# Scan phase of a hybrid SSD and Conformer block: decay weights shared with ScalarE, weight rows loaded earlier, and the first modulation vector and five gate pairs moved between phases

## The chip, the cores and the metric

The kernel runs on one core of one Trainium2 chip. The metric is the time of one execution on the device in microseconds (us); the time of a kernel is the median of its runs. The profile comes from one profiled execution.

## The reference

One layer of a diffusion backbone: 256 latent tokens and 256 context tokens of width 2048, float32. The parts that matter here:

```python
proj = h @ w_in                     # split into z, xbc, dt_raw, glu, gates
xbc = jax.nn.silu(dwconv_seq(xbc, conv_w, conv_b))
dt = jax.nn.softplus(dt_raw + dt_bias)
...
    cs = jnp.cumsum(da_c, axis=1)                 # in a chunk of 128 tokens
    seg = cs[:, :, None] - cs[:, None, :]
    decay = jnp.exp(jnp.where(lower, seg, -jnp.inf))
    cb = jnp.einsum("blgn,bsgn->blsg", c_c, b_c)
    y_diag = jnp.einsum("blsgj,bsgjp->blgjp", cb[..., None] * decay, xdt_c)
    y_off = jnp.einsum("blgn,bgjpn->blgjp", c_c, h) * jnp.exp(cs)[..., None]
...
y_a = rmsnorm(y * jax.nn.silu(z), ssm_norm) @ w_proj_a
y_b = cf @ w_proj_b                               # cf: the Conformer branch
x = x + g1 * ((sigmoid(g_a) * y_a + sigmoid(g_b) * y_b) @ w_out)
x = x + g2 * swiglu(modulate(rmsnorm(x, norm_ffn), sh2, sc2))
```

The scan runs forward and backward over the tokens, for 8 groups of 8 heads (64 wide, state 128). The six modulation vectors (shift, scale and gate of each sub-layer) are `silu(c) @ w_mod + b_mod`; the two that the first input needs are made in phase 0, the other four (g1, sh2, sc2, g2; 2048 numbers each) are those called `modvec(0)` to `modvec(3)` below.

## The kernel before

**Weight stream.** Weights come in tiles of 512 KB (`w32`, L102), issued on SP's queue in program order into 6 buffers. `split` (L109) makes two tiles of each: `wh`, a rounded copy by ScalarE (ACT, L113), and `wl`, the rest, by VectorE (DVE, L114). A tile is a "unit": for a pair of column tiles TensorE (PE) runs 16 matmuls on it (L151 with 512 columns, L153 with 256), or 24 with 512 columns where context and latents are both needed (L143, L144, L146). `wh` and `wl` have 4 buffers each. The program is scheduled ahead of time; each engine then runs its instructions in a fixed order, in which the two halves of `split` have a raised priority.

**Phases.** Phase 0 (to about 250 us) norms, modulates and makes the first projections. Phase A (to about 932 us) is the scan. Phase B (to about 1295 us) makes 16 pairs of the Conformer input (`f`) and 16 gate pairs (8 for `ga`, 8 for `gb`); phase C multiplies by w_proj_b and w_proj_a; D by w_out (to about 1672 us), E and F are the feed-forward part.

**Phase A.** A loop over 8 stages; stage s scans group s-1 with `ssd` (L533) and meanwhile runs projections: `bcpair` and `xpair` of later groups, `zpair` (L689) of groups whose scan is finished. `ssd` is a generator of 15 steps; the loop takes a step each time that the projections' running time, by a table of estimates, has passed the next fifteenth. In the last stage the steps are spread over all units but the last 8. In `ssd`, `diag` (L607) makes the weights of half the heads of a chunk: `cs` (512 KB, the cumulative sums sent to all partitions by a DMA, 2 buffers) is shifted by ACT (L614) and by DVE (L617, which also takes the minimum of the two directions), ACT takes the exponential (L619), POOL and DVE make `w` from the products C·B of both directions (L621, L624), and L626 multiplies. PE then uses it (L633, `ydiag`), and L662 to L669 add the carried state, scaled by `ec` (another broadcast DMA), to `yfm`. `zpair` gates `yfm` with z, adds the squares to `yss` on POOL (L701), scales by `ssm_norm` on DVE (L703) and writes `yg` to DRAM.

**The modulation vectors.** `modvec` (L480) loads 32 tiles of w_mod (the "rows") through the same 6 buffers and adds each to `mac` on DVE (L489, L491), without PE. A hook after each unit takes its steps: `modvec(0)` 34 steps in 116 units of phase A, `modvec(1)` and `modvec(2)` 68 steps in 246 units of B, C and D, `modvec(3)` in phase E.

Of the kernel before, what the change touches and what calls it, by code (L numbers as in the profile page):

```python
# [62 lines left out]
def _block(top, tc, nc, x, c, ctx_in, c_ctx, w_mod, b_mod, norm_mix, w_in, conv_w, conv_b,  # L63
# [162 lines left out]
    def xct():  # L226
        return pa1.tile([P, 512], F32, tag="xc", name="xc", bufs=8)
# [24 lines left out]
    cst = pa1.tile([P, 2, P], F32, name="cst")  # L252
    ncs = pa1.tile([P, 2, 64], F32, name="ncs")
# [4 lines left out]
    def dt_chain(dt_raw, scr):  # L258
# [44 lines left out]
        V.tensor_copy(out=cst.rearrange("p a b -> p (a b)"), in_=b[:, 0:256])  # L303
        V.tensor_scalar(out=ncs, in0=cst[:, :, 0:64], scalar1=-1.0, scalar2=None, op0=ALU.mult)
# [175 lines left out]
    def modvec(slot, pl):  # L480
        """One of the other four modulation vectors, off the tensor engine; a step per unit."""
        o = slot + 2
        for h in range(D // UB):
            ac = pl.tile([P, UB], F32, tag="mac", name="mac", bufs=1)
            for k in range(KD):
                c0 = o * D + h * UB
                wt = w32([(lambda t: t, w_mod[k * P:(k + 1) * P, c0:c0 + UB])])
                if k == 0:
                    V.tensor_scalar(out=ac, in0=wt, scalar1=silc[:, k:k + 1], scalar2=None, op0=ALU.mult)  # L489
                else:  # L490
                    V.scalar_tensor_tensor(out=ac, in0=wt, scalar=silc[:, k:k + 1], in1=ac, op0=ALU.mult, op1=ALU.add)  # L491
                yield
            yield
# [26 lines left out]
    # ------------------------------------------------------------ phase A  # L520
    with pool("pa2", "right") as pa:
# [11 lines left out]
        def ssd(g, xts, Bt, Ct, res):  # L533
            """The two scans of group g, a step per yield; the output goes feature-major to res."""
            gs = slice(8 * g, 8 * g + 8)
            csb, ecb = {}, {}

            def cs_load(cc, half):
# [4 lines left out]
                csb[cc, half] = t  # L543
# [545 lines left out]
```

## Time and profile before

| | us |
|---|---|
| median of 3 runs | 2440.6 |
| lowest and highest run | 2436.62, 2441.51 |
| span of the profiled execution | 2437.1 |
| TensorE busy in it | 2355.9 |
| VectorE busy | 1672.2 |
| ScalarE busy | 1194.6 |
| GpSimd busy | 153.2 |

The span runs from the first to the last instruction of the profiled execution. Its own time is that span, as far as the profile shows it, and it lies 3.5 us under the median and inside the runs. The difference between the span and TensorE's busy time, 81.2 us, is all the time in which TensorE stands idle.

### The profile page before, as it was taken

The page shows a single profiled execution, that of the slowest core. Times are in us where ns is not written, and L with a number is a line of the kernel's source. Part 1 is how long each engine was busy: PE and PEld are TensorE (multiplying, and loading weights), DVE is VectorE, ACT ScalarE, POOL GpSimd, SP SyncE. Part 2 cuts the span into 40 slices and gives each one's busy share as a digit, 9 for nine tenths or more (in the row PEclk, how much of TensorE's full clock was granted, in tenths as well). Part 3 has the DMA queues.
Part 4 walks back from the last instruction along what each step waited for, and adds up shares of the span by engine and source line. Part 5 has one row for each costly group of instructions (what it writes and reads, how often), then busy time and mean ns, then how long its engine had stood idle before and what let it go on. Part 6 is the DMA issues. An engine that isn't in the chain of part 4 may idle for free.

```text
span 2437.1 us, 35157 instructions
## 1 busy us (share of the span) xinstructions
PE 2355.9 (97%) x13400; PEld 1981.7 (81%) x13400; DVE 1672.2 (69%) x2343; ACT 1194.6 (49%) x1700; POOL 153.2 (6%) x181
## 2 busy tenths in 40 slices
PE   6999899999999999999999999999999999999998
PEld 3668687878777778888888888887888888888888
DVE  4659887877777887878757666667666566655554
ACT  4335546546444565545755444445444444444443
POOL 1000010100100111013000000000000000000000
PEclk9999999999999999999999999999999999999999
DMA  9994556655655567776777777785777677766663
GB/s 274 292 298 116 133 170 182 180 156 166 182 155 159 178 195 238 237 238 208 234 249 250 241 252 237 242 264 182 232 221 226 214 226 229 219 197 193 194 192 113
DMA packets 468458, 509.41 MB, mean 209 GB/s; under 512 B 18148, under 2 KB 438195, under 8 KB 467777
## 3 DMA queue, kind: packets, MB, share of 16 engines
q1 hardware_dynamic: 461936, 488.74, 65.5%
q0 software_dynamic: 5792, 17.35, 2.2%
q8 instruction: 105, 1.72, 0.3%
q10 hardware_dynamic: 560, 1.08, 0.1%
q14 instruction: 65, 0.52, 0.1%
HBM read 496.35 MB, written 10.75 MB: 208 GB/s over the span
## 4 chain that ended last, share of the span: by engine, by line
PE 76%; DMA 4%; DVE 4%; issue 2%; ACT 1%; SPq 0%; POOL 0%; DVEq 0%; ACTq 0%; POOLq 0%
PE acc L151 38%; PE acc L153 21%; PE acc L143 4%; PE acc L146 4%; PE acc L144 3%; DMA w<-in_w_mod_dram 2%; PE acc L155 2%; DMA cs<-cs_d 2%; DVE wl L114 2%; PE ss L662 1%; PE ss L633 1%; DVE xc L245 0%; PE tp L556 0%; PE ss L641 0%; ACT wh L113 0%
## 5 line engine op out<-in xcount | busy, mean ns | idle before, releaser
L114 DVE TENSOR_TENSOR wl<-w,wh 128x1024 fp32r<-128x1024 f32 (+3 forms) x702 | 839.4, 1200 | 412.9 <-ACT wh L113 411.3
L113 ACT CAST wh<-w 128x1024 fp32r<-128x1024 f32 (+3 forms) x702 | 717.8, 1024 | 728.0 <-PE acc L151 450.1
L151 PE MATMUL acc<-hx,wh 128*128 128x512 f32 x1556 | 433.8, 397 | 0.0
L151 PE MATMUL acc<-h,wh 128*128 128x512 f32 x1320 | 366.7, 396 | 4.4 <-DVE h L973 2.4
L151 PEld LDWEIGHTS acc<-hx,wh 128*128 128x128 f32 x1556 | 272.4, 189 | 41.8 <-issue 3.4
L153 PEld LDWEIGHTS acc<-hx,wl 128*128 128x128 f32 x1664 | 255.0, 188 | 38.3 <-DVE wl L114 1.8
L143 PE MATMUL acc<-hx,wh 128*128 128x512 f32 x656 | 267.8, 409 | 3.0 <-ACT wh L113 2.4
L153 PE MATMUL acc<-hx,wl 128*128 128x256 f32 x1664 | 267.4, 282 | 1.4 <-DVE wl L114 1.4
L491 DVE SCALAR_TENSOR_TENSOR mac<-w,silc,mac 128x1024 f32<-128x1024 f32 x120 | 156.5, 1304 | 162.8 <-DMA w<-in_w_mod_dram 162.4
L151 PEld LDWEIGHTS acc<-h,wh 128*128 128x128 f32 x1320 | 231.5, 190 | 38.2 <-issue 5.3
L144 PE MATMUL acc<-hx,wh 128*128 128x512 f32 x656 | 259.9, 397 | 0.0
L153 PEld LDWEIGHTS acc<-h,wl 128*128 128x128 f32 x1408 | 216.1, 189 | 30.1
L153 PE MATMUL acc<-h,wl 128*128 128x256 f32 x1408 | 223.9, 281 | 0.0
L146 PE MATMUL acc<-hx,wl 128*128 128x512 f32 x656 | 185.2, 395 | 0.0
L151 PE MATMUL acc<-hid,wh 128*128 128x512 f32 x602 | 166.3, 396 | 0.0
L143 PEld LDWEIGHTS acc<-hx,wh 128*128 128x128 f32 x656 | 124.3, 190 | 39.9 <-issue 8.5
L146 PEld LDWEIGHTS acc<-hx,wl 128*128 128x128 f32 x656 | 124.5, 190 | 27.2 <-issue 0.4
L144 PEld LDWEIGHTS acc<-hx,wh 128*128 128x128 f32 x656 | 124.9, 190 | 25.9 <-issue 2.1
L151 PE MATMUL acc<-yg,wh 128*128 128x512 f32 x496 | 136.4, 395 | 0.4 <-ACT wh L113 0.4
L151 PEld LDWEIGHTS acc<-hid,wh 128*128 128x128 f32 x602 | 103.6, 189 | 13.8
L153 PEld LDWEIGHTS acc<-hid,wl 128*128 128x128 f32 x616 | 94.3, 189 | 13.1
L153 PE MATMUL acc<-hid,wl 128*128 128x256 f32 x616 | 98.0, 281 | 0.0
(346 smaller groups left out, 2722.7 us busy)
## 6 DMA issues: line engine op xcount, KB each, us to landing
w<-in_w_in_dram SPq DMA_DIRECT2D x248, 512.0 KB, 4.5
w<-in_w_mod_dram SPq DMA_DIRECT2D x192, 512.0 KB, 4.8
w<-in_w_ffn_gate_dram SPq DMA_DIRECT2D x88, 512.0 KB, 4.6
w<-in_w_ffn_up_dram SPq DMA_DIRECT2D x88, 512.0 KB, 4.6
w<-in_w_ffn_down_dram SPq DMA_DIRECT2D x88, 512.0 KB, 3.5
w<-in_w_proj_a_dram SPq DMA_DIRECT2D x64, 512.0 KB, 4.7
w<-in_w_in_dram SPq DMA_DIRECT2D x74, 256.0 KB, 3.8
cs<-cs_d SPq DMA_DIRECT2D x32, 512.0 KB, 6.0
```

Source lines behind the costliest of these rows:

```text
L113: A.copy(out=hi[:, :n], in_=t[:, :n])
L114: V.tensor_tensor(out=lo[:, :n], in0=t[:, :n], in1=hi[:, :n].bitcast(F32), op=ALU.subtract)
L143: E.matmul(o, wj(hi, k), act(kofs + k)[:, 0, :ncol], start=kofs + k == kbeg, stop=False)
L144: E.matmul(o, wj(hi, k), act(kofs + k)[:, 1, :ncol], start=False, stop=False)
L146: E.matmul(o, wj(lo, k), act(kofs + k)[:, 0, :ncol], start=False, stop=last and k == nk - 1)
L151: E.matmul(o2, wj(hi, k), act(kofs + k)[:, :, :T], start=kofs + k == kbeg, stop=False)
L153: E.matmul(o[:, :T], wj(lo, k), act(kofs + k)[:, 0, :T], start=False, stop=last and not hold)
L155: E.matmul(o2, wj(hi, nk - 1), act(kofs + nk - 1)[:, :, :T], start=False, stop=True)
L491: V.scalar_tensor_tensor(out=ac, in0=wt, scalar=silc[:, k:k + 1], in1=ac, op0=ALU.mult, op1=ALU.add)
L633: E.matmul(ydp[r:r + 64, (hd // 2) * P:(hd // 2 + 1) * P], xs[:, cc, hd * 64:(hd + 1) * 64], e[:, j * P:(j + 1) * P], start=True, stop=True)
L662: E.matmul(yo[:, i * P:(i + 1) * P], hs_[r][:, i * P:(i + 1) * P], Ct[:, cc * P:(cc + 1) * P], start=True, stop=True)
```

## The change

- `diag`: ACT shifts both directions (8 instructions of 128x128 in place of 4), DVE takes the minimum in one instruction of 128x512 in place of four (was L617). The products of the backward direction go to a tile `w2` by four ACT instructions, and DVE adds `w` and `w2` in one 128x512 instruction in place of four (was L624).
- `zpair`: the sum `yss` moves from POOL to DVE (16 instructions), the scaling by `ssm_norm` from DVE to ACT (32).
- `cs` of the next group is loaded as soon as the second chunk of a group frees its buffer, not at the group's start; `ec_load(0)` is issued at the start of `ssd`; `diag(1, 0)` is written two steps later.
- `modvec` loads a row one step ahead of the one that it adds. `modvec(0)` leaves phase A; B, C and D now take 102 steps in 226 units.
- z of group 4, 5 and 6 is made a stage sooner (stages 6, 7, 8), and five of the `ga` pairs (20 units) are made in stages 7 and 8 instead of in phase B; `xc` gets a ninth buffer, since their results lie there until phase B's tiles exist.

```diff
 def modvec(slot, pl):
...
-            for k in range(KD):
-                c0 = o * D + h * UB
-                wt = w32([(lambda t: t, w_mod[k * P:(k + 1) * P, c0:c0 + UB])])
-                if k == 0:
-                    V.tensor_scalar(out=ac, in0=wt, scalar1=silc[:, k:k + 1], scalar2=None, op0=ALU.mult)
-                else:
-                    V.scalar_tensor_tensor(out=ac, in0=wt, scalar=silc[:, k:k + 1], in1=ac, op0=ALU.mult, op1=ALU.add)
+            c0 = o * D + h * UB
+            wn = None
+            for k in range(KD + 1):
+                wt = wn
+                if k < KD:
+                    wn = w32([(lambda t: t, w_mod[k * P:(k + 1) * P, c0:c0 + UB])])
+                if k == 1:
+                    V.tensor_scalar(out=ac, in0=wt, scalar1=silc[:, 0:1], scalar2=None, op0=ALU.mult)
+                elif k > 1:
+                    V.scalar_tensor_tensor(out=ac, in0=wt, scalar=silc[:, k - 1:k], in1=ac, op0=ALU.mult,
+                                           op1=ALU.add)
                 yield
-            yield
...
 def diag(cc, half):
...
                 for j in range(4):
-                    A.activation(out=t4[:, 0, j], in_=t4[:, 0, j], func=AF.Identity, bias=ncs[:, cc, hs + j:hs + j + 1])
-                e, tb = t[:, 0], t[:, 1]
-                for j in range(4):
-                    V.scalar_tensor_tensor(out=t4[:, 0, j], in0=t4[:, 1, j], scalar=c3[:, 1, j:j + 1], in1=t4[:, 0, j],
-                                           op0=ALU.subtract, op1=ALU.min)
-                A.activation(out=e, in_=e, func=AF.Exp)
-                w = ptile([P, 512], "w")
+                    for r in range(2):
+                        A.activation(out=t4[:, r, j], in_=t4[:, r, j], func=AF.Identity,
+                                     bias=ncs[:, cc, r * 64 + hs + j:r * 64 + hs + j + 1])
+                e = t[:, 0]
+                V.tensor_tensor(out=e, in0=e, in1=t[:, 1], op=ALU.min)
+                w, w2 = ptile([P, 512], "w"), ptile([P, 512], "w2")
...
                 for j in range(4):
-                    V.scalar_tensor_tensor(out=m4(w)[:, j], in0=cbb[:, cc, :], scalar=dtT[:, cc, 64 + hs + j:64 + hs + j + 1],
-                                           in1=m4(w)[:, j], op0=ALU.mult, op1=ALU.add)
+                    A.activation(out=m4(w2)[:, j], in_=cbb[:, cc, :], func=AF.Identity,
+                                 scale=dtT[:, cc, 64 + hs + j:64 + hs + j + 1])
+                A.activation(out=e, in_=e, func=AF.Exp)
+                V.tensor_tensor(out=w, in0=w, in1=w2, op=ALU.add)
                 V.tensor_tensor(out=e, in0=e, in1=w, op=ALU.mult)
...
                 if cc == 0:
-                    cs_load(1, half)
+                    cs_load(g, 1, half)
+                elif g + 1 < G:
+                    cs_load(g + 1, 0, half)
...
-            G_.tensor_tensor(out=yss, in0=yss, in1=sz, op=ALU.add)
+            V.tensor_tensor(out=yss, in0=yss, in1=sz, op=ALU.add)
             for i in range(2):
-                V.tensor_scalar(out=yg[:, i, :], in0=yg[:, i, :], scalar1=vec("ssm_norm", 4 * g + 2 * j + i),
-                                scalar2=None, op0=ALU.mult)
+                A.activation(out=yg[:, i, :], in_=yg[:, i, :], func=AF.Identity,
+                             scale=vec("ssm_norm", 4 * g + 2 * j + i))
...
+        def gpair(j):
+
+            a = acc2()
+            for k0 in range(0, KD, UK):
+                hi, lo = unit_cols(w_in, k0, UK, [(OFF_GLU + j * 256, 256)])
+                mm_unit(a, hi, lo, UK, k0, KD, [0, 0], hxa)
+                yield
+            early.append(fold(a, xct().rearrange("p (i t) -> p i t", i=2)))
         for stage in range(1, G + 1):
             zs = [(zpair(gg, j, yr[gg]), 2.56) for gg in
-                  {2: [0], 3: [1], 4: [2], 5: [3], 7: [4], 8: [5, 6, 7]}.get(stage, []) for j in range(2)]
+                  {2: [0], 3: [1], 4: [2], 5: [3], 6: [4], 7: [5], 8: [6, 7]}.get(stage, []) for j in range(2)]
+            gs_ = [(gpair(j), 2.56) for j in {7: [0], 8: [1, 2, 3, 4]}.get(stage, [])]
...
-                tasks += zs
+                tasks += zs[:2] + gs_ + zs[2:]
...
-                    if stage > 1:
-                        g1hook()
...
-                if stage == G and n == 3:
+                if stage == G and n == 5:
...
-    hook = bg(mgen, 68, 246)
+    hook = bg(mgen, 102, 226)
```

What this makes of the engines' orders stands below at three places. First VectorE in phase A, where the scan of the fourth group is in its second chunk: from `cs` and `y` (L668, L669) to the gating of a z pair (L699). Before:

```order
L617 SCALAR_TENSOR_TENSOR cs<-cs,cst 128x128
L668 TENSOR_TENSOR y<-ss,ec 128x512
L114 TENSOR_TENSOR wl<-w_5096,wh 128x1024
L669 TENSOR_TENSOR yfm<-yfm,y 128x4x128
L617 SCALAR_TENSOR_TENSOR cs<-cs,cst 128x128 x3
L624 SCALAR_TENSOR_TENSOR w<-cbb,dtT,w 128x128 x2
L114 TENSOR_TENSOR wl<-w_5135,wh 128x1024
L624 SCALAR_TENSOR_TENSOR w<-cbb,dtT,w 128x128 x2
L161 TENSOR_TENSOR sz<-sz,acc 128x256
L626 TENSOR_TENSOR cs<-cs,w 128x512
L161 TENSOR_TENSOR sz<-sz,acc 128x256
L699 TENSOR_TENSOR yg<-yfm,sz 128x512
```

And VectorE at the same place after the change (L621 is the minimum, L629 the sum of `w` and `w2`, L630 the product, L673 and L674 are `y` and `yfm`, L704 the gating):

```order
L621 TENSOR_TENSOR cs<-cs 128x512
L673 TENSOR_TENSOR y<-ss,ec 128x512
L621 TENSOR_TENSOR cs<-cs 128x512
L674 TENSOR_TENSOR yfm<-yfm,y 128x4x128
L630 TENSOR_TENSOR cs<-cs,w 128x512
L114 TENSOR_TENSOR wl<-w_5097,wh 128x1024
L629 TENSOR_TENSOR w<-w,w_4990 128x512
L114 TENSOR_TENSOR wl<-w_5136,wh 128x1024
L630 TENSOR_TENSOR cs<-cs,w 128x512
L161 TENSOR_TENSOR sz<-sz,acc 128x256 x2
L704 TENSOR_TENSOR yg<-yfm,sz 128x512
L114 TENSOR_TENSOR wl<-w_5185,wh 128x1024
```

Eight short instructions per half chunk have become two of 128x512, and they stand between more of the other work. The second place is VectorE in phase C, in the first products with w_proj_a; `mac` is the sum of a modulation vector, `fc` a result of the product. Before:

```order
L491 SCALAR_TENSOR_TENSOR mac<-w_12776,silc,mac 128x1024
L114 TENSOR_TENSOR wl<-w_12668,wh 128x1024
L161 TENSOR_TENSOR fc<-fc,acc 128x256
L114 TENSOR_TENSOR wl<-w_12690,wh 128x1024
L161 TENSOR_TENSOR fc<-fc,acc 128x256
L919 TENSOR_TENSOR fc<-ga,fc 128x512
L114 TENSOR_TENSOR wl<-w_12732,wh 128x1024
L920 TENSOR_TENSOR fc<-fc,gb 128x512
L491 SCALAR_TENSOR_TENSOR mac<-w_12845,silc,mac 128x1024
L114 TENSOR_TENSOR wl<-w_12754,wh 128x1024
```

After:

```order
L493 SCALAR_TENSOR_TENSOR mac<-w_13883,silc,mac 128x1024
L114 TENSOR_TENSOR wl<-w_13839,wh 128x1024
L161 TENSOR_TENSOR fc<-fc,acc 128x256
L114 TENSOR_TENSOR wl<-w_13861,wh 128x1024
L161 TENSOR_TENSOR fc<-fc,acc 128x256
L493 SCALAR_TENSOR_TENSOR mac<-w_13930,silc,mac 128x1024
L114 TENSOR_TENSOR wl<-w_13886,wh 128x1024
L931 TENSOR_TENSOR fc<-ga,fc 128x512
L932 TENSOR_TENSOR fc<-fc,gb 128x512
L114 TENSOR_TENSOR wl<-w_13908,wh 128x1024
```

A row of w_mod now comes after every second `wl`, where before it came after every third or fourth. The third place is TensorE in the last stage of phase A, around the transposes of a scan's step (L556, after the change L558). Before:

```order
L153 MATMUL acc<-hx,wl 128x256
L633 MATMUL ss<-cs,xs 64x128 x8
L153 MATMUL acc<-hx,wl 128x256 x3
L151 MATMUL acc<-hx,wh 128x512 x4
L153 MATMUL acc<-hx,wl 128x256 x2
L662 MATMUL ss<-Ct,h_6845 128x128 x4
L662 MATMUL ss<-Ct,hb 128x128 x4
L153 MATMUL acc<-hx,wl 128x256 x2
L556 MATMUL tp<-ident,xc 128x128 x4
L151 MATMUL acc<-hx,wh 128x512 x3
L153 MATMUL acc<-hx,wl 128x256 x3
L593 MATMUL tp<-Ct,Bt 128x128 x2
```

After:

```order
L558 MATMUL tp<-ident,Bt 128x128 x4
L558 MATMUL tp<-ident,xc 128x128 x4
L151 MATMUL acc<-hx,wh 128x512 x4
L153 MATMUL acc<-hx,wl 128x256 x4
L151 MATMUL acc<-hx,wh 128x512 x4
L153 MATMUL acc<-hx,wl 128x256 x4
L558 MATMUL tp<-ident,xc 128x128 x4
L151 MATMUL acc<-hx,wh 128x512 x4
L153 MATMUL acc<-hx,wl 128x256 x4
L151 MATMUL acc<-hx,wh 128x512 x4
L153 MATMUL acc<-hx,wl 128x256 x4
```

The steps of the scan stand further apart: before, the matmuls of four of them (L633 and L662 of one group, L556 and L593 of the next) within about one unit of 16 matmuls; after, a whole unit between one and the next.

## Rows read from the trace of the kernel before

**Rows 1.** The page, part 1: busy us of each engine, share of span.

```profile
PE 2355.9 (97%) x13400; PEld 1981.7 (81%) x13400; DVE 1672.2 (69%) x2343; ACT 1194.6 (49%) x1700; POOL 153.2 (6%) x181
```

**Rows 2.** Windows: stretch, us, busy by engine (count), PEclk, DMA share, GB/s.

```profile
250.00:312.00 62.00, 55.26 (x264) 41.62 (x264) 49.35 (x93) 35.74 (x66) 4.16 (x4) 0.94 0.52 136
312.00:707.00 395.00, 389.26 (x2003) 316.03 (x2001) 305.69 (x484) 207.41 (x308) 38.59 (x32) 1.00 0.61 176
707.00:932.00 225.00, 211.78 (x1148) 170.47 (x1149) 179.31 (x294) 118.13 (x183) 29.15 (x26) 0.98 0.59 171
932.00:1292.00 360.00, 358.64 (x2054) 312.32 (x2053) 270.60 (x358) 200.72 (x270) 39.03 (x34) 1.00 0.76 233
1292.00:1672.00 380.00, 370.18 (x2138) 322.02 (x2137) 257.50 (x302) 173.39 (x224) 17.22 (x32) 0.99 0.77 248
1760.00:2400.00 640.00, 640.00 (x3682) 558.26 (x3681) 374.76 (x417) 296.31 (x376) 4.30 (x8) 1.00 0.68 211
```

**Rows 3.** Windows: the last two stages of phase A, and B to D.

```profile
782.00:932.00 150.00, 141.13 (x818) 115.15 (x818) 126.58 (x205) 87.26 (x134) 25.00 (x22) 1.00 0.64 185
...
932.00:1672.00 740.00, 728.82 (x4191) 634.34 (x4189) 528.10 (x659) 374.11 (x493) 56.25 (x66) 1.00 0.76 241
```

**Rows 4.** What PE waited for, 707 to 932: us, times, longest.

```profile
PE tp L556 <- ACT btok L576: 4.0, 2, 3.1
PE ss L662 <- DVE yfm L678: 3.8, 3, 1.9
```

**Rows 5.** The chain that ended last, 740 to 890: start, us, what.

```profile
744.98 5.60 DMA cs<-cs_d
...
768.13 6.84 DMA w<-in_w_mod_dram
...
775.74 0.69 DVE yfm L678
776.47 1.75 PE ss L662 x8
```

**Rows 6.** Windows of two stretches at half clock.

```profile
708.60:712.00 3.40, 3.40 (x11) 2.73 (x10) 2.52 (x3) 0.32 (x1) 0.00 (x0) 0.50 0.38 108
776.90:780.30 3.40, 3.40 (x13) 2.92 (x12) 3.40 (x7) 1.28 (x4) 0.00 (x0) 0.50 0.81 201
```

**Rows 7.** Lines by form, 250 to 910: busy us, mean ns, idle before.

```profile
L614 ACT ACTIVATE cs<-cs,ncs 128x128 f32<-128x128 f32 x128 | 41.8, 391 | 68.4 <-DMA cs<-cs_d 68.4
L617 DVE SCALAR_TENSOR_TENSOR cs<-cs,cst 128x128 f32<-128x128 f32 x128 | 40.1, 354 | 36.6 <-ACT cs L614 36.6
L624 DVE SCALAR_TENSOR_TENSOR w<-cbb,dtT,w 128x128 f32<-128x128 f32 x128 | 38.1, 344 | 7.6 <-POOL w L621 7.6
L626 DVE TENSOR_TENSOR cs<-cs,w 128x512 f32<-128x512 f32 x32 | 21.9, 684 | 0.4
L703 DVE TENSOR_SCALAR yg<-yg,vt 128x256 f32<-128x256 f32 x26 | 18.4, 743 | 0.0
L113 ACT CAST wh<-w 128x1024 fp32r<-128x1024 f32 x126 | 131.5, 1044 | 104.4 <-PE acc L144 52.1 <-PE acc L151 35.6 <-PE acc L155 10.6
```

**Rows 8.** What ACT waited for, 707 to 932.

```profile
ACT cs L614 <- DMA cs<-cs_d: 20.9, 7, 5.5
```

**Rows 9.** Lines on DVE, 932 to 1672 (B, C and D).

```profile
L114 DVE TENSOR_TENSOR wl<-w,wh 128x1024 fp32r<-128x1024 f32 x257 | 316.1, 1240 | 82.9 <-ACT wh L113 82.6
L491 DVE SCALAR_TENSOR_TENSOR mac<-w,silc,mac 128x1024 f32<-128x1024 f32 x60 | 78.2, 1304 | 109.9 <-DMA w<-in_w_mod_dram 109.8
```

**Rows 10.** Timeline of SP's queue, 1340 to 1376: a row's issue.

```profile
1347.09 0.34 SPq L106 DMA_DIRECT2D w<-in_w_mod_dram  x1
```

**Rows 11.** Timeline of DVE, 1340 to 1366, what follows that issue.

```profile
1352.62 1.28 DVE L491 SCALAR_TENSOR_TENSOR mac<-w,silc,mac 128x1024 f32<-128x1024 f32 x1 [3.77 <-DMA w<-in_w_mod_dram]
```

**Rows 12.** DMA issues of w_mod, 932 to 1672: KB, median us to landing.

```profile
w<-in_w_mod_dram SPq DMA_DIRECT2D x64, 512.0 KB, 4.7
```

**Rows 13.** The same, 1672 to 2200 (phase E).

```profile
w<-in_w_mod_dram SPq DMA_DIRECT2D x31, 512.0 KB, 3.7
```

More of the change, by code (lines that the diff above doesn't have):

```diff
@@ L210, in vecr @@
         return vt[:, o:o + n]
+    early = []
     dsk = cpool.tile([P, 64], F32, name="dsk")
@@ L226, in xct @@
     def xct():
-        return pa1.tile([P, 512], F32, tag="xc", name="xc", bufs=8)
+        return pa1.tile([P, 512], F32, tag="xc", name="xc", bufs=9)
     def bt():
@@ L251, in _block @@
     dtT = pa1.tile([P, 2, P], F32, name="dtT")
-    cst = pa1.tile([P, 2, P], F32, name="cst")
-    ncs = pa1.tile([P, 2, 64], F32, name="ncs")
+    ncs = pa1.tile([P, 2, P], F32, name="ncs")
     dcol = pa1.tile([P, 32], F32, name="dcol")
@@ L302, in dt_chain @@
             E.transpose(out=b[:, i * P:(i + 1) * P], in_=csf[:, i * P:(i + 1) * P], identity=ident)
-        V.tensor_copy(out=cst.rearrange("p a b -> p (a b)"), in_=b[:, 0:256])
-        V.tensor_scalar(out=ncs, in0=cst[:, :, 0:64], scalar1=-1.0, scalar2=None, op0=ALU.mult)
+        V.tensor_scalar(out=ncs.rearrange("p a b -> p (a b)"), in0=b[:, 0:256], scalar1=-1.0, scalar2=None, op0=ALU.mult)
         b = tpb()
@@ L535, in ssd, with cs_load @@
             gs = slice(8 * g, 8 * g + 8)
-            csb, ecb = {}, {}
-            def cs_load(cc, half):
+            ecb = {}
+            def cs_load(g, cc, half):
                 hs = 8 * g + 4 * half
@@ L542, in cs_load @@
                 nc.sync.dma_start(out=t, in_=src.partition_broadcast(P))
-                csb[cc, half] = t
+                csb[g, cc, half] = t
             def ec_load(cc):
@@ L565, in weigh @@
                 return xw
-            cs_load(0, 0)
-            cs_load(0, 1)
+            if g == 0:
+                cs_load(0, 0, 0)
+                cs_load(0, 0, 1)
+            ec_load(0)
             btok = ptile([P, 4, P], "btok")
@@ L652, in ssd @@
             e1 = diag(0, 1)
-            ec_load(0)
             yield
@@ L671, in ssd @@
                 ydiag(ydp, e0, cc, 0)
-                if cc == 0:
-                    e0 = diag(1, 0)
                 yield
@@ L680, in ssd @@
                 yo = yoff(1)
+                if cc == 0:
+                    e0 = diag(1, 0)
                 yield
@@ L763, in _block @@
                 pass
-        for _ in g1gen:
-            pass
-    pas.close()
     gbs = ExitStack()
@@ L773, in _block @@
     rsta = gbp.tile([P, T], F32, name="rsta")
+    for j, t in enumerate(early):
+        A.activation(out=ga[:, 2 * j:2 * j + 2, :], in_=t, func=AF.Sigmoid)
+    pas.close()
     macs = ExitStack()
@@ L797, in mods @@
     def mods():
-        for slot in (1, 2):
+        for slot in (0, 1, 2):
             yield from modvec(slot, macp)
     mgen = mods()
-    hook = bg(mgen, 68, 246)
+    hook = bg(mgen, 102, 226)
     cfs = ExitStack()
@@ L865, in _block @@
             t = t[:, 2 * o:2 * o + 2, :]
-            fold(pair(w_in, OFF_GLU + j * 256, KD, hxa, hook), t)
-            A.activation(out=t, in_=t, func=AF.Sigmoid)
+            if j >= len(early):
+                fold(pair(w_in, OFF_GLU + j * 256, KD, hxa, hook), t)
+                A.activation(out=t, in_=t, func=AF.Sigmoid)
+                if j > len(early):
+                    next(ln, None)
             if j < 8:
                 V.tensor_tensor(out=t, in0=t, in1=rsta.unsqueeze(1).to_broadcast([P, 2, T]), op=ALU.mult)
-            if j > 0:
-                next(ln, None)
         for _ in ln:
```

6 lines of the change are left out of this document (2 added, 4 removed).

## The prediction

> **What bounds the kernel now.** I read the page's busy times first, then the windows by phase, then PE's waits and the chain where PE stands idle, then the lines for prices. PE is busy for 2355.9 us [rows 1], and the change gives it the same number of matmuls. So the span, 2437.1 us, can only lose what PE idles, 81.2 us, and the matmul time that a half clock adds. The windows say where the idle time lies [rows 2]: 62.00 - 55.26 = 6.7 us in the first scan stage, 395.00 - 389.26 = 5.7 in stages 2 to 5, 225.00 - 211.78 = 13.2 in stages 6 to 8, 1.4 in phase B, 9.8 in C and D, nothing in 640 us of phase E. The remaining 44 us are phase 0, the passage from D to E, and the end, which the change leaves alone. What it can win lies in the scan.
>
> In stages 6 to 8 PE waits for the scan's own results (`btok`, `yfm`), not for weights [rows 4]. The chain shows what makes them late [rows 5]: a `cs` transfer of 5.60 us, then DVE standing behind a row of w_mod for 6.84 us, and only then `yfm` on DVE and L662 on PE. DVE runs in order, so a row that has not landed holds back every scan step behind it. After two such pauses PE's granted clock is 0.50, its 1.2 GHz level, for 3.4 us each time [rows 6]; work done there at 2.4 GHz would take half of it, so each costs about 1.7 us.
>
> **The change, part by part.**
>
> *The decay weights.* Each of the 32 half chunks drops four L617 and four L624 from DVE: 4 x 0.354 + 4 x 0.344 = 2.79 us [rows 7]. It gets two instructions of 128x512, priced as L626, also a two-input instruction of that size: 2 x 0.684 = 1.37. DVE gains 1.4 us per half chunk, 45 us in all. ACT gets eight more of 128x128 at L614's 0.391: 3.1 us per half chunk, 100 us in all. The scaled copies of `cbb` have no row; L614 has the same shape and function, so it stands for them. *The z pairs* drop two L703 (1.49 us) from DVE and add one sum like L626 (0.68): 0.8 us less for each of 16, 13 us. ACT pays two copies of 128x256, between L614's 0.391 and twice that, so about 1 us per pair. None of this is on PE's path by itself: it counts where DVE or ACT keeps PE waiting.
>
> The Trainium skill speaks against the first part: "ScalarE: Activation LUTs", Rules for kernel authors, puts plain additions and multiplications on VectorE. The rows agree that ACT is dearer, 3.1 us paid for 1.4 gained; "Perfetto Trace Analysis", Optimizing Scalar/DVE Operations, would still offload where VectorE is saturated, and what the first rule would make of the time is the rival on ScalarE.
>
> *Stages 7 and 8.* Before, the last stage spread 15 scan steps over 24 - 8 = 16 units; now 4 z pairs and 4 gate pairs make 32 - 8 = 24. A unit takes 640.00 x 16 / 3682 = 2.78 us [rows 2], so that the scan has 67 us of matmul cover instead of 44. In these two stages DVE was busy 126.6 us beside 141.1 us of PE work [rows 3]. After: minus 8 half chunks x 2.79 (22), plus 8 x 1.37 (11), minus the rows of w_mod (four at 1.30, 5), plus 20 `wl` at 1.24 [rows 9] and 10 folds (29 together), minus two z pairs that are made earlier (8 `wl`, their folds and L703: 16), minus 6 x 0.8 for the z pairs that stay (5): about 118 us. PE has 20 - 8 = 12 more units, 33 us: 118 beside 174, from 90% to 68%. ACT goes from 87.3 to 87 + 8 x 3.1 (25) + 6 z pairs (6) + 20 `wh` at 1.04 [rows 7] with folds (25) - 12 for the two z pairs = 131 beside 174; with the 20.9 us that it waited for `cs` [rows 8], 152, or 87%. So both engines have room, and the moved units are work that hides the scan's chain.
>
> *Loads.* `cs` of a group's first chunk comes a few steps before use, and `diag(1, 0)` stands two steps behind its load. In a scan stage of some 99 us (395.00 / 4) two of 15 steps are 13 us, over the 5.60 us of the transfer [rows 5]; but ACT's order is fixed by the scheduler, which may put the use right behind the arrival again, so I keep the waits of [rows 8] in the sum above and take no gain.
>
> *No rows in phase A* removes 32 x 1.30 = 42 us of DVE work and every wait of the kind at 768 us.
>
> For the scan I take: of 5.7 + 13.2 us idle, 14 go and 5 stay (`btok`, `xs` hang on transposes and ACT whatever DVE does); two half-clock stretches go, 3.4 us. The first stage stays: DVE gains there what ACT loses. Bounds: nothing, if ACT takes DVE's place; all of 5.7 + 13.2 + 6.7 + 3.4 = 29.
>
> *32 more rows in B, C and D.* Before, 64 rows stood in 728.8 us of PE work [rows 3], 11.4 us each. DVE worked 528.1 us there, 81 of them on rows, so 447 on the rest, and waited 109.8 us for rows, 1.7 us per row [rows 9]: (447 + 81 + 110) / 728.8 = 88% taken. After: 96 rows in 728.8 - 20 x 2.78 = 673 us, 7.0 us each; the rest of the work is 447 - 29 = 418, or 4.35 per row, and with 1.30 for the row itself 5.65 are taken. So a row may make DVE wait 1.36 us before DVE, not PE, sets the pace.
>
> What will the wait be? The transfer: rows landed in 4.7 us here at 241 GB/s [rows 3, 12] and in 3.7 us in phase E at 211 [rows 2, 13], 1 us more for 30 GB/s. The demand becomes 241 x 740 = 178 MB, plus 32 - 20 = 12 tiles (6 MB), over some 684 us: 269 GB/s, so I estimate 5.6 us. A row of phase C, issued at 1347.09, was added from 1352.62, after a wait of 3.77 us [rows 10, 11]. Against that, the load now stands a step ahead of its use, which puts one more `wl` or so of work (1.24) between issue and use: 1.7 + 0.9 - 1.2 = 1.4 us, just at the limit. Nothing is lost on average, but in stretches with more other work (phase C with its `yg` parts) DVE will fall short. I take +4 us; bounds: -4 if the lead hides the transfers and even small waits of PE in B to D go; and, if the lead gains nothing, (1.7 + 0.9 - 1.36) x 96 = 119 us, which bounds it only in principle, since a DVE that falls behind also demands less; with the wait as it was, (1.7 - 1.36) x 96 = 33 us, which I take as the practical end.
>
> In phase E the rows come earlier too, but PE never idles there: 0. The work that hides them is PE's own.
>
> **Sum.** -14 (scan idle) - 3.4 (clock) + 4 (rows) = -13.4: a span of 2423.7 us. The median of the runs lies 3.5 us above the profiled span; carried over, 2427.2, say 2427 us.
>
> **The rivals.** 0.2% of the time, 4.9 us, is about what a measurement of this kernel can tell from no change.
>
> 1. *The forecast*, 2420 to 2434 us: the scan's idle time goes, the rows cost a little. Chance 0.45.
>
> 2. *The lead hides the rows altogether.* DVE's 110 us of waiting shrink, B to D have fewer gaps than before and the scan gives most of its 29 us: 2440.6 - 25 - 4 = 2412 us. For it: E, where rows land in 3.7 us [rows 13]. Against it: the demand of 269 GB/s. Chance 0.15.
>
> 3. *Slower: DVE becomes the bound in B to D.* The place is each `mac` in C and B; the price is (wait per row - 1.36) x 96 us. It eats the scan's 17 us at 1.36 + 17 / 96 = 1.54 us per row, and at the old 1.7 us it costs 33: 2440.6 - 17 + 33 = 2457 us. For it: [rows 10, 11], 5.5 us from issue to use, and a third more DVE time per unit of PE for rows. Against it: the lead. Chance 0.2.
>
> 4. *No change: ScalarE takes VectorE's place in the scan.* ACT's 152 of 174 us reach the limit if its `cs` waits double. In stages 6 to 8 they were 7 waits of up to 5.5 us [rows 8], and 68.4 us over the whole scan [rows 7]. Then the scan's idle time stays and the rows' +4 is balanced by the rows' absence there: 2437 to 2442. Chance 0.2.
>
> The first and second are faster by over 0.2%; so is a part of the fourth, where the scan gives half: together 0.63. The same: 0.17. Slower: 0.2. The range from 2405 to 2450 holds the first, the fourth, nearly all of the second and the nearer part of the third.
>
> **What would show it.** Right: PE idle in stages 2 to 8 under 8 us, no row of w_mod in the scan's chain, few half-clock stretches there; `mac`'s waits in B to D about 1.4 us per row and PE waiting for `wl` (L153) for less than 10 us. Wrong: PE waits for `wl` in C for tens of us with DVE over 95% busy or waiting for rows; or L662 and L556 still wait, now behind ACT's `cs` and `w2`. Step by step, I am least sure of the rows' landing time, which I have extrapolated from two stretches that differ in more than their demand.

## The result and the profile after

The changed kernel takes 2409.36 us (median of 4 runs, 2406.11 to 2410.64); beside it the kernel before took 2440.86 us. The ratio is 0.987, with a 95% interval from 0.985 to 0.989: faster by 31.5 us, where 13.4 were forecast. The profiled execution's span is 2407.9 us, 29.2 less than before.

The page's busy times, as in [rows 1]:

```profile
PE 2346.0 (97%) x13400; PEld 1976.3 (82%) x13400; DVE 1639.7 (68%) x2134; ACT 1266.5 (53%) x1980; POOL 131.2 (5%) x165
```

The idle time fell from 81.2 to 2407.9 - 2346.0 = 61.9 us, and the same 13400 matmuls are 9.9 us less busy. So there are two terms: 19.3 us of waiting and 9.9 us of shorter matmuls. Most of the second is half clock that is gone: between 240 and 1310 us the kernel before has five stretches of 3.4 us at a granted clock of 0.50 (from 262, 299, 709, 777 and 1299 us), some 8.5 us of lost time, and the changed kernel has none there. Where the rest comes from was not traced.

Windows of the changed kernel: the first scan stage, stages 2 to 5, stages 6 to 8, B and the start of C, the rest of C and D. Columns as in [rows 2].

```profile
241.50:302.20 60.70, 58.94 (x292) 45.27 (x292) 53.33 (x81) 49.28 (x104) 4.15 (x4) 1.00 0.49 131
302.20:691.00 388.80, 388.80 (x2002) 317.15 (x2002) 264.45 (x353) 242.20 (x451) 26.66 (x24) 1.00 0.53 148
691.00:974.90 283.90, 281.72 (x1578) 234.98 (x1578) 198.37 (x256) 181.80 (x330) 19.56 (x20) 1.00 0.60 173
974.90:1267.20 292.30, 287.89 (x1656) 249.88 (x1654) 251.01 (x337) 169.14 (x234) 39.75 (x34) 1.00 0.84 267
1267.20:1643.30 376.10, 367.18 (x2132) 318.74 (x2133) 273.51 (x317) 171.42 (x222) 16.12 (x30) 1.00 0.85 272
```

The stages have other lengths now, so here are the windows of the kernel before, cut at the same events (the first transposes of a group's B; the first copy of an `f` pair; the first matmul of phase E): the first stage, stages 2 to 5, stages 6 to 8, and B to D.

```profile
239.30:307.90 68.60, 61.86 (x292) 47.04 (x292) 55.36 (x108) 36.65 (x66) 4.16 (x4) 0.95 0.49 128
307.90:702.70 394.80, 390.92 (x2012) 317.72 (x2011) 304.89 (x483) 208.96 (x311) 38.59 (x32) 1.00 0.61 175
702.70:940.70 238.00, 222.91 (x1213) 179.91 (x1212) 190.48 (x307) 124.73 (x190) 31.39 (x28) 0.99 0.58 171
940.70:1673.10 732.40, 720.12 (x4140) 626.72 (x4138) 522.27 (x655) 370.80 (x491) 54.01 (x65) 1.00 0.76 241
```

Three things are to be seen. The first stage, with the same 292 matmuls, is 68.60 - 60.70 = 7.9 us shorter, and its clock goes from 0.95 to 1.00. Stages 2 to 5 took 702.7 - 307.9 = 394.8 us and take 388.80, without any idle time. Of these 6.0 us, 3.9 were idle time; the other 2.1 are ten matmuls of `modvec(0)` (2012 against 2002) that went to B to D with its rows, so they are no gain. Stages 6 to 8 idle 283.90 - 281.72 = 2.2 us in place of 15.1. B to D idle 13.3 us (4.4 + 8.9) in place of 12.3: 32 more rows of w_mod cost about 1 us.

Of what PE waited for in the scan, 241 to 975 us, little is left (compare [rows 4], of a third of it):

```profile
PE tp L558 <- ACT btok L580: 1.2, 1, 1.2
PE ss L637 <- DVE cs L630: 1.2, 2, 0.9
PE ss L637 <- PE acc L144: 0.9, 1, 0.9
PE ss L667 <- DVE y L673: 0.3, 1, 0.3
```

What DVE waited for from 975 to 1643 us, and the landing of the rows there, which answer to [rows 9, 12]:

```profile
DVE mac L493 <- DMA w<-in_w_mod_dram: 91.9, 47, 4.9
```

```profile
w<-in_w_mod_dram SPq DMA_DIRECT2D x92, 512.0 KB, 4.8
```

Rows land in 4.8 us at 270 GB/s, against 4.7 at 241. The wait is 91.9 / 92 = 1.0 us per row, where 1.4 was forecast and 1.36 was the limit. ScalarE's waits for `cs` in the scan, before 68.4 us [rows 7], are now 28.0 us in stages 2 to 8 and 2.6 in the first:

```profile
ACT cs L618 <- DMA cs<-cs_d: 28.0, 14, 4.1
```

### The profile page after: what moved, and what is told of

Read it like the earlier page. It is cut to its first block, busy times and chain, and to the rows that moved or that the text cites. A ratio compares the mean times of both kernels' runs of the same rounds, so it can differ in the third digit from the quotient of the medians.

```text
span 2407.9 us, 35235 instructions
## 1 busy us (share of the span) xinstructions
PE 2346.0 (97%) x13400; PEld 1976.3 (82%) x13400; DVE 1639.7 (68%) x2134; ACT 1266.5 (53%) x1980; POOL 131.2 (5%) x165
## 4 chain that ended last, share of the span: by engine, by line
PE 84%; DMA 7%; issue 4%; DVE 4%; ACT 2%; POOL 0%; SPq 0%; DVEq 0%; ACTq 0%; POOLq 0%
PE acc L151 38%; PE acc L153 20%; PE acc L143 6%; PE acc L144 6%; PE acc L146 6%; DMA w<-in_w_mod_dram 4%; PE acc L155 2%; DVE wl L114 2%; PE ss L667 1%; DMA cs<-cs_d 1%; PE ss L637 1%; PE tp L558 1%; PE ss L370 1%; DMA w<-in_w_in_dram 1%; DMA yst<-yg_d 1%
## 5 line engine op out<-in xcount | busy, mean ns | idle before, releaser
L618 ACT ACTIVATE cs<-cs,ncs 128x128 f32<-128x128 f32 x256 | 81.6, 390 | 32.4 <-DMA cs<-cs_d 30.6
```

Source lines behind the costliest of these rows:

```text
L618: A.activation(out=t4[:, r, j], in_=t4[:, r, j], func=AF.Identity, bias=ncs[:, cc, r * 64 + hs + j:r * 64 + hs + j + 1])
```

## The experiments

Each ratio is to runs of the kernel before on the same chip, with its 95% interval; the changed kernel's is 0.987 [0.985, 0.989] above and 0.986 [0.984, 0.988] on another chip. Windows and waits are of one profiled run each, the ratios of all runs.

**Parts of the change taken back.** First the load ahead:

```diff
-            for k in range(KD + 1):
-                wt = wn
-                if k < KD:
-                    wn = w32([...])
+            for k in range(KD):
+                wt = w32([...])
```

> The changed kernel, but each row of w_mod is loaded in the step that adds it (no step ahead), in B to E. Theory A (the lead is what kept the 32 more rows from costing time): the wait per row in B to D goes from 91.9 / 92 = 1.0 us back to 1.7 us or more, over the 1.36 us that VectorE can spare, PE waits for wl there, and the kernel takes 2440 us or more (+30). Theory B (the rows landed in 4.8 us even at 270 GB/s, so there was room anyway): 0 to +6 us, 2409 to 2415.

Measured: 2412.97 us, ratio 0.985 [0.983, 0.987], span 2403.8. Theory B holds: the load ahead is worth nothing. VectorE waits 90.6 us for rows without it and 91.9 with it. Why is seen in the order of VectorE's instructions: put side by side in the two traces, 2095 of its 2134 stand in the same order with and without the lead. One step in the program's text hardly moved them.

Then the decay weights back to VectorE (eight 128x128 instructions in `diag` as before; the second product too, which is left out of the cut below):

```diff
-                    for r in range(2):
-                        A.activation(out=t4[:, r, j], ...)
-                V.tensor_tensor(out=e, in0=e, in1=t[:, 1], op=ALU.min)
+                    A.activation(out=t4[:, 0, j], ...)
+                for j in range(4):
+                    V.scalar_tensor_tensor(out=t4[:, 0, j], in0=t4[:, 1, j], scalar=c3[:, 1, j:j + 1], ...)
```

> The changed kernel, but the decay weights are made as before: the second shift with the minimum and the second product by VectorE in 128x128 pieces. Theory A (VectorE's load was what held up the scan): about 45 us more VectorE work in 32 half chunks bring back a third of the scan's gain, +8 to +10 us, 2418. Theory B (the rows' pauses and the missing cover held it up; VectorE is 70% busy in the scan now): within 3 us of 2409, ScalarE 100 us less busy.

Measured: 2409.42 us, 0.985 [0.983, 0.986]. Theory B again. Only the first stage shows it (below, then stages 2 to 8):

```profile
240.90:304.10 63.20, 59.17 (x293) 45.25 (x293) 54.77 (x105) 36.38 (x67) 5.88 (x4) 1.00 0.47 126
304.10:974.50 670.40, 669.74 (x3574) 551.59 (x3572) 485.07 (x777) 360.33 (x560) 42.55 (x44) 1.00 0.56 159
```

It is 2.5 us longer than in the changed kernel; stages 2 to 8 idle 0.7 us.

Then the scan's loads:

```diff
-            if g == 0:
-                cs_load(0, 0, 0)
-                cs_load(0, 0, 1)
-            ec_load(0)
+            cs_load(g, 0, 0)
+            cs_load(g, 0, 1)
...
-                elif g + 1 < G:
-                    cs_load(g + 1, 0, half)
...
             e1 = diag(0, 1)
+            ec_load(0)
...
                 ydiag(ydp, e0, cc, 0)
+                if cc == 0:
+                    e0 = diag(1, 0)
...
-                if cc == 0:
-                    e0 = diag(1, 0)
```

> The changed kernel, but with the scan's loads as before: ec of the first chunk issued after the second half's weights, cs of a group's first chunk at the group's start, the third set of weights directly behind the load it needs. Theory A (the first stage was held up by ec's 5.66 us, 292 to 298 us in the chain, and its clock by that pause): the first stage gets back its 6.7 us of idle time, other stages little: +6 to +9 us, 2417. Theory B (the first stage got faster because VectorE had less to do): within 3 us of 2409, the first stage 61 us long.

Measured: 2410.76 us, 0.985 [0.983, 0.986]; the first stage takes 60.3 us. Theory A falls: with the decay weights shared, the loads may come late.

```profile
242.50:302.80 60.30, 58.73 (x292) 45.34 (x291) 52.69 (x82) 48.67 (x103) 4.15 (x4) 1.00 0.59 136
```

Then the cover:

```diff
-                  ... 5: [3], 6: [4], 7: [5], 8: [6, 7]}
-            gs_ = [(gpair(j), 2.56) for j in {7: [0], 8: [1, 2, 3, 4]}.get(stage, [])]
-    hook = bg(mgen, 102, 226)
+                  ... 5: [3], 7: [4], 8: [5, 6, 7]}
+            gs_ = [(gpair(j), 2.56) for j in {}.get(stage, [])]
+    hook = bg(mgen, 102, 246)
```

> The changed kernel, but z of groups 4 to 6 a stage later again and no gate pairs in the scan (16 in phase B, 102 steps in 246 units). Theory A (the last stages idled because too little matmul work covered them): stages 6 to 8 idle 8 to 13 us again with one or two half-clock stretches: +8 to +14 us, 2417 to 2423. Theory B (they idled because of the rows in VectorE's order): under 4 us of idle time in stages 6 to 8, and B to D have 56 us more to cover the rows: within 3 us of 2409.

Measured: 2439.69 us, 0.998 [0.996, 1.000]: nearly the whole gain is gone, more than theory A asked for. And not where it looked for it. Windows of this run: stages 6 to 8, and B to D.

```profile
691.40:919.70 228.30, 217.88 (x1202) 176.88 (x1201) 162.79 (x220) 151.72 (x291) 18.10 (x20) 1.00 0.55 159
919.70:1674.00 754.30, 728.97 (x4161) 631.42 (x4159) 559.11 (x689) 371.75 (x493) 54.13 (x64) 0.99 0.81 256
```

Stages 6 to 8 idle 10.4 us and keep their clock. B to D idle 25.3 us, with a clock of 0.99, although they hold 20 units more to cover the same rows. VectorE waits there for rows for 128.5 us, and PE for `wl`:

```profile
DVE mac L493 <- DMA w<-in_w_mod_dram: 128.5, 59, 4.7
```

```profile
PE acc L153 <- DVE wl L114: 9.5, 8, 2.6
PE acc L151 <- DVE cfx L896: 4.9, 1, 4.9
```

Against the changed kernel two things are new there: the five gate pairs, and the rows' spacing, one step in 2.41 units in place of 2.22. The same kernel with the old spacing tells that apart:

```diff
-    hook = bg(mgen, 102, 246)
+    hook = bg(mgen, 102, 226)
```

> The run without cover (16 gate pairs in phase B, z a stage later), but with the rows as dense as in the change, 102 steps in 226 units instead of 246. Theory A (B to D were 20 us longer there because one row in 2.4 units falls worse into the six buffers than one in 2.2: VectorE waited 1.37 us per row against 1.0): B to D fall to some 730 us and the kernel to 2418 to 2424. Theory B (B to D were longer for another reason, the gate pairs' place): it stays at 2435 to 2442, or rises with the denser rows.

Measured: 2417.61 us, 0.990 [0.988, 0.992]. Stages 6 to 8, then B to D, and DVE's waits for rows:

```profile
686.40:912.50 226.10, 217.93 (x1204) 177.05 (x1203) 163.09 (x220) 152.05 (x292) 18.10 (x20) 1.00 0.56 160
912.50:1644.10 731.60, 721.41 (x4160) 628.19 (x4158) 561.88 (x689) 374.09 (x493) 55.70 (x64) 1.00 0.83 264
```

```profile
DVE mac L493 <- DMA w<-in_w_mod_dram: 65.9, 45, 3.8
```

Theory A: B to D are 754.3 - 731.6 = 22.7 us shorter with *denser* rows, 15.1 of it idle time (25.3 against 10.2) and 7.6 PE's busy time, at a granted clock of 1.00 in place of 0.99. This profiled run is the fastest of its five; the medians differ by 22.1 us too. A rival is that with 226 units the rows end 20 units earlier and leave the end of D free. It is not that: in a stretch of phase C in which both runs have rows, the run with 246 idles 11.2 us in 217 and the one with 226 next to nothing:

```profile
1283.00:1500.00 217.00, 205.80 (x1147) 176.94 (x1148) 148.44 (x166) 94.53 (x121) 7.53 (x14) 0.98 0.79 252
1276.00:1493.00 217.00, 216.85 (x1246) 188.35 (x1245) 163.96 (x178) 100.06 (x126) 7.53 (x14) 1.00 0.85 278
```

What is left of the cover's worth is the idle time of stages 6 to 8, 8.2 us here and 10.4 in the run before, against 2.2, and the difference between 0.990 and 0.987, whose intervals overlap.

**Parts of the change done alone on the kernel before.** The loads (with `diag(1, 0)` two steps later, as in the change):

```diff
-            cs_load(0, 0)
-            cs_load(0, 1)
+            if g == 0: ...                    # cs of the first group only
+            ec_load(0)
...
-            ec_load(0)                        # from behind diag(0, 1)
...
+                elif g + 1 < G:
+                    cs_load(g + 1, 0, half)
```

> The kernel before, with the scan's loads of the change alone: ec of the first chunk issued at the start of a group's scan, cs of the next group as its buffer comes free, the third set of weights two steps behind its load. Theory A (the scan idles because ec and cs land late): the first stage loses its 6.7 us of idle time and its two half-clock stretches, later stages some: -8 to -14 us, 2430. Theory B (undoing these loads in the changed kernel cost nothing, so they are worth something only while VectorE is held up by rows): -3 to -8 us, and nearly all of it in the first stage, which has no rows. Theory C (worth nothing anywhere): within 3 us.

Measured: 2432.47 us, 0.998 [0.996, 0.999]: theory B. The first stage takes 64.0 us, 4.6 less, and one of its two half-clock stretches stays; stages 6 to 8 still idle 12.4:

```profile
237.60:301.60 64.00, 60.23 (x293) 45.81 (x292) 53.94 (x104) 36.18 (x66) 5.02 (x4) 0.97 0.46 132
...
693.60:929.60 236.00, 223.64 (x1213) 180.96 (x1212) 190.27 (x306) 124.58 (x190) 32.58 (x28) 0.98 0.59 172
```

The shared work (the second product stays on VectorE; `yss` and `ssm_norm` are shared as in the change):

```diff
-                    V.scalar_tensor_tensor(out=t4[:, 0, j], ...)          # four of 128x128
+                V.tensor_tensor(out=e, in0=e, in1=t[:, 1], op=ALU.min)    # one of 128x512
```

> The kernel before with the work between the engines shared as in the change, as far as its memory allows: the shifts of both directions on ScalarE and one minimum of 128x512 on VectorE, yss on VectorE, ssm_norm on ScalarE; the second product stays on VectorE, since there is no room for its tile. Rows stay in phase A. Theory A (the first stage is held up by VectorE's load and the others by rows): the first stage 4 to 8 us shorter, the others within 3 us: -4 to -9 us. Theory B (VectorE's load is what delays every stage): -12 us or more, spread over the stages.

Measured: 2432.6 us, 0.995 [0.993, 0.997]; its runs spread from 2425.46 to 2438.04, and its profiled span is 2436.2. The first stage, then stages 2 to 5 and 6 to 8:

```profile
244.70:305.20 60.50, 58.94 (x293) 45.27 (x293) 52.83 (x93) 45.18 (x89) 4.16 (x4) 1.00 0.56 142
305.20:698.10 392.90, 390.26 (x2012) 317.52 (x2011) 292.18 (x423) 233.84 (x394) 29.28 (x24) 1.00 0.59 177
698.10:931.10 233.00, 220.21 (x1213) 178.91 (x1212) 178.41 (x268) 145.42 (x248) 18.68 (x20) 0.99 0.59 174
```

Neither theory holds as it stands. The time, 13 us less by the ratio, is theory B's "-12 us or more". The stages lie between the two: the first gets back 8.1 us, as in theory A, and stages 2 to 8 are 1.9 + 5.0 us shorter, over its 3; they still idle 15.4 us together, against 19.0. The profiled run is the slowest of the six, and its B to D are longer than before, so where the median's gain lies is not fully shown.

The rows, moved to B to D, in both spacings:

```diff
-        g1gen = modvec(0, pa)
-        g1hook = bg(g1gen, 34, 116)
-        for slot in (1, 2):
-    hook = bg(mgen, 68, 246)
+        for slot in (0, 1, 2):
+    hook = bg(mgen, 102, 246)                 # 102, 226 in the second run
```

> The kernel before, with the rows of the first modulation vector moved from phase A to B to D alone (102 steps in 246 units, no load ahead, no gate pairs in A). Theory A (rows in VectorE's order are what delays the scan): stages 2 to 8 idle 8 us less and lose their half-clock stretches, -10 to -15 us there, and B to D become 15 to 30 us longer as in the run without cover: 2436 to 2450 in all, so no gain or a loss. Theory B (the scan idles for its own chain): the scan stays within 4 us, and the time becomes 2455 to 2465.

> The kernel before with its rows moved to B to D alone, but 102 steps in 226 units where the earlier such run had 246. Theory A (the rows' spacing made B to D longer there, and the scan had gained): B to D 15 to 22 us shorter than in that run, 2420 to 2428 in all, so this one part carries more than half of the change's gain. Theory B (spacing matters only together with the other parts): 2438 to 2445.

Measured: 2443.77 us, 1.002 [1.000, 1.004], with 246, and 2424.52 us, 0.992 [0.990, 0.994], with 226. Theory A both times. Stages 2 to 5 and 6 to 8, then B to D, of the run with 226:

```profile
305.10:693.90 388.80, 388.80 (x2002) 317.15 (x2001) 287.79 (x460) 210.46 (x313) 35.17 (x32) 1.00 0.51 148
693.90:924.40 230.50, 219.42 (x1204) 177.87 (x1203) 178.99 (x293) 119.68 (x187) 32.77 (x28) 0.99 0.53 157
924.40:1656.10 731.70, 720.96 (x4160) 627.32 (x4158) 561.39 (x689) 372.90 (x493) 56.05 (x64) 1.00 0.82 264
```

With 246, B to D:

```profile
928.90:1676.80 747.90, 727.93 (x4161) 630.43 (x4159) 559.29 (x689) 371.79 (x493) 55.33 (x65) 0.99 0.81 258
```

Without rows, stages 2 to 5 have no idle time, whatever else is as before; stages 6 to 8 idle 11.1 us with 226 and 11.3 with 246. The spacing decides whether that is given back: 731.70 us in B to D with one, 747.90 with the other.

The cover alone, with rows still in the scan (four gate pairs, not five; the rows' spacing changes a little with it, 34 steps in 132 units and 68 in 230):

```diff
-                  ... 7: [4], 8: [5, 6, 7]}
+                  ... 6: [4], 7: [5], 8: [6, 7]}
+            gs_ = [(gpair(j), 2.56) for j in {8: [0, 1, 2, 3]}.get(stage, [])]
```

> The kernel before, with the cover of the change alone: z of groups 4 to 6 a stage sooner and four gate pairs (not five, the tiles for a fifth do not fit) in the last stage, rows of the first vector still in phase A (34 steps in 132 units), 68 steps in 230 units after it. Theory A (cover hides the scan's chain whatever makes it late): stages 6 to 8 idle 8 to 10 us less and lose their half-clock stretches: -10 to -14 us, 2427. Theory B (rows are the cause, cover only helps with them gone): within 4 us of before.

Measured: 2436.9 us, 0.999 [0.997, 1.000]: theory B. Stages 6 to 8 idle 281.40 - 273.48 = 7.9 us, half as much as before, but two half-clock stretches stay, and stages 2 to 5 and the first one keep their waits.

```profile
704.70:986.10 281.40, 273.48 (x1512) 226.14 (x1511) 220.27 (x336) 147.34 (x221) 33.20 (x28) 0.99 0.64 187
```

**Denser rows in the changed kernel.** Beside it, on the same chip, the changed kernel itself.

```diff
-    hook = bg(mgen, 102, 226)
+    hook = bg(mgen, 102, 196)
```

> The changed kernel itself, for a comparison on the same chip: both theories say the ratio to before that it had, 0.985 to 0.989.

> The changed kernel with denser rows, 102 steps in 196 units instead of 226. Theory A (VectorE stands at a row because its order takes the row before weight tiles that were loaded ahead of it, and with more rows in the six buffers a row's buffer comes free earlier): the waits for rows in B to D fall from 92 to some 60 us and the small gaps of TensorE there go: -2 to -5 us against the changed kernel. Theory B (more demand in a shorter stretch makes rows land later and VectorE the bound): +5 to +20 us.

Measured: the changed kernel 2411.22 us, 0.986 [0.984, 0.988]; denser 2407.92 us, 0.984 [0.982, 0.987]. The waits for rows fell from 90.2 to 52.9 us:

```profile
DVE mac L493 <- DMA w<-in_w_mod_dram: 52.9, 39, 3.0
```

Theory B falls, and theory A holds for the waits. But B to D take 668.0 us with denser rows and 667.6 without, so the waits that went had cost nothing any more. The runs of the two do not overlap (2403.86 to 2408.67, and 2409.74 to 2411.66), while the intervals of the ratios do: whether the 3 us are a gain is not settled.

## Why the prediction was right in sign and too small

*What bounds the kernel*: right. The matmuls are the same, and all of the gain is idle time and half clock, nearly all of it in the scan. The measured time lies inside the range, but the sum was too small by more than a factor of two, and no single term accounts for that; the largest is the first stage. The measured time comes nearest to the second rival's 2412 us, and that is luck: its cause, a lead that hides the rows, was worth nothing in the run without it.

*The first stage, "DVE gains there what ACT loses": this step failed.* It was taken as 0 and measured as -7.9 us, 5.0 of idle time and 2.9 of half clock. That is no noise: in the four profiled runs whose first stage is as before it takes 66.6 to 69.4 us, in the six looked at that share the decay weights 60.3 to 61.5. I had the mean load of two engines in mind, where two chains decide. PE's waits in the first stage of the kernel before were:

```profile
PE tp L556 <- ACT xs L587: 3.6, 1, 3.6
PE ss L662 <- DVE y L668: 1.9, 1, 1.9
PE ss L662 <- DVE yfm L678: 1.3, 1, 1.3
```

The largest one hangs on ScalarE's order. Before, a shift of the second `cs` tile stood ahead of the copy `xs` that PE needs, and waited for its transfer; with both directions of the first tile on ScalarE, shifts of the first tile stand there. Two rows of ScalarE before, then the shifts of the changed kernel at the same place:

```profile
259.61 0.40 ACT L614 ACTIVATE cs<-cs,ncs 128x128 f32<-128x128 f32 x1 [1.59 <-DMA cs<-cs_d]
...
260.95 0.56 ACT L587 COPY xs<-tp 128x512 f32<-128x512 f32 x1
```

```profile
258.27 1.57 ACT L618 ACTIVATE cs<-cs,ncs 128x128 f32<-128x128 f32 x5 [1.29 <-DMA cs<-cs_d]
```

The second hangs on VectorE's order. The chain of the kernel before, 290 to 300 us, shows it:

```profile
290.80 0.26 DVE cs L617
291.07 0.60 DVE y L668
291.67 0.27 DVE cs L617
291.94 0.34 SPq L550
...
292.33 5.66 DMA ec<-ec_d
...
298.11 0.70 DVE y L668
...
298.86 1.98 PE ss L662 x8
```

`ec` has one buffer; the next `ec` is issued only when `y` has read the last one, and `y` stands among the L617 of another half chunk. The loads alone remove this second pause, and the first stays (64.0 us); sharing alone removes both (60.5 us). So undoing either one in the changed kernel costs 2.5 us at most. Neither order was changed by an experiment of its own, without the rest of the sharing.

*The scan's idle time, "14 go and 5 stay"*: right in kind, too small. Cut at the same events, 3.9 + 15.1 us were idle, and 2.2 stay. The runs part the causes. In stages 2 to 5 it is the rows: moved alone, they leave 388.80 us without a gap, and VectorE had waited 22.2 us for rows there. In stages 6 to 8 the rows' going takes 15.1 us of idle time to 11.1. Sharing and loads on top of that take it to between 8.2 and 10.4 (two runs with the same scan, so their part is within the spread), and the cover to 2.2. What the rows did in stages 6 to 8 is not shown, and *the reading of [rows 5], "DVE standing behind a row of w_mod for 6.84 us", was wrong*. VectorE waited for rows for only 1.0 us in stages 6 to 8; the waits for rows, 308 to 703 and 703 to 941 us:

```profile
DVE mac L491 <- DMA w<-in_w_mod_dram: 22.2, 12, 3.8
```

```profile
DVE mac L491 <- DMA w<-in_w_mod_dram: 1.0, 1, 1.0
```

What held VectorE up ahead of `yfm` at 775.7 us was L617, which waited 4.68 us for ScalarE's L614, which had waited 5.50 us for `cs`; the row itself is added only behind `yfm`, at 776.9 us. With the rows gone and nothing else changed, the same wait is still there, 4.43 us, and PE's pause behind it is 1.4 us in place of 1.9. The row before the change, then the one with the rows moved (226):

```profile
772.78 1.23 DVE L617 SCALAR_TENSOR_TENSOR cs<-cs,cst 128x128 f32<-128x128 f32 x4 [4.68 <-ACT cs L614]
```

```profile
758.57 1.23 DVE L617 SCALAR_TENSOR_TENSOR cs<-cs,cst 128x128 f32<-128x128 f32 x4 [4.43 <-ACT cs L614]
```

"Both engines have room" was right: ACT was busy 181.8 of 283.9 us in stages 6 to 8, so the rival on ScalarE did not come. Nor does the rule of the Trainium skill, "ScalarE: Activation LUTs", Rules for kernel authors, that plain arithmetic belongs on VectorE, decide here: ScalarE was busy 1266.5 us in place of 1194.6, and in the scan PE waited for it only 1.2 us. In the changed kernel sharing is worth nothing in stages 2 to 8 (0.7 us idle without it).

*The clock, -3.4 us*: too small. It counted the two stretches of [rows 6]; the two of the first stage and one behind phase B went as well.

*The rows, +4 us: the landing time failed.* It was extrapolated to 5.6 us from two stretches at 241 and 211 GB/s; at 270 it was 4.8. What differs between those stretches is more than their demand, as the last sentence of the prediction feared. *"The load now stands a step ahead"* failed too: it changed hardly anything in the order and nothing in the time. And the limit of 1.36 us per row was the wrong test. It is a mean: in the run without cover the wait was 128.5 / 96 = 1.34 us per row, VectorE had 754.3 - 559.1 = 195 us without work, and still 22.7 us were lost against the same work in the other spacing. The waits come in clusters. In that run PE waited eight times for `wl`; before five of the eight, rows had held VectorE for 7.3 to 10.1 of the last 25 us, where the mean of B to D is 4.3. That a cluster empties PE's buffers is the likely reading; before the other three waits there was no cluster.

*Where the waits come from*: VectorE's order takes a row before weight tiles that were loaded ahead of it. The rows of the order shown with the change say so by their numbers, which grow in the order of loading: before, `mac` reads w_12776 and then come `wl` of w_12668, w_12690 and w_12732; after, w_13883 stands ahead of w_13839 and w_13861. The overtaken tiles still hold some of the six buffers, so that the row, it is argued, is issued late. The traces let them be counted, from the order of loads on SP's queue and the order of use on VectorE in B to D:

| run | units for its steps | tiles overtaken per row | wait per row, us |
|---|---|---|---|
| before | 246 for 68 | 3.2 | 1.7 |
| no cover | 246 for 102 | 2.4 | 1.3 |
| rows moved alone | 246 for 102 | 2.4 | 1.2 |
| changed kernel | 226 for 102 | 2.0 | 1.0 |
| rows moved alone | 226 for 102 | 2.0 | 0.7 |
| no cover | 226 for 102 | 1.9 | 0.7 |
| changed kernel, denser | 196 for 102 | 1.5 | 0.55 |

Within a run it is the same: in the changed kernel the seven rows that overtake four tiles wait 3.6 us on average, those that overtake three 1.4, two 0.6, and one or none nothing. So the overtaking goes with the wait, row by row, though not alone: 2.0 tiles come with 1.0 us in one run and 0.7 in another. A kernel with another order and the same spacing was not tried.

In sum, against the forecast of -13.4 us for the span: the first stage -7.9 in place of 0; idle time in stages 2 to 8 -16.8 (3.9 + 12.9) in place of -14; PE's busy time from stage 2 to the end of D -8.3, of which three half-clock stretches explain 5.1, in place of -3.4; idle time in B to D +1.0 in place of +4; the phases outside, +2.8 in place of 0. That makes the -29.2 measured.

## What to carry to other kernels

Take work that waits for a transfer out of an in-order engine's queue where a chain runs through that queue, and put it where the chain isn't; here that was worth some 0.8% by itself, but only in one of two spacings. A mean of slack per item doesn't tell whether a wait costs: look at the order and at clusters. A step of the critical chain that names a transfer need not have held up the engine: look in that engine's own rows for what it waited for. Several parts of a change that cure the same stall look worthless when each is undone alone, so do each alone on the old kernel as well.

## What the runs showed of the hardware that was not expected

Rows of 512 KB landed in medians of 4.6 to 5.0 us at 257 to 270 GB/s (4.8 in the changed kernel at 270; without cover 5.0 at 257 and 4.6 at 261), hardly later than the 4.7 at 241 GB/s.

In the scan of the kernel before, four pauses of PE of 1.9 to 3.6 us (they end at 262, 299, 708 and 776 us) were each followed by 3.4 us at a granted clock of 0.50; two others, of 2.4 us (to 512) and 3.2 us (to 857), were not. In the changed kernel no pause in the scan is longer than 1.2 us, and the whole scan, 241 to 975 us, ran at 1.00.
